# Squares of the latents summed by one-column matmuls in the second layer, and a last output block in narrower pieces

## The chip, the cores and the metric

The kernel runs as one program on one core of a Trainium2 chip. The metric is the device time of one execution in microseconds (us). The five engines named below are PE (TensorE, the matmuls), DVE (VectorE), ACT (ScalarE), POOL (GpSimd) and SP (SyncE, which here only starts DMAs). The kernel before was timed at 1753.45, 1750.38 and 1753.22 us, a median of 1753.22 us.

## The reference

Two layers of one mixer each, on a sequence of 1024 tokens of 1024 values. Per layer:

```
h = x * (1 + scale) + shift                      # scale, shift, gate from the conditioning c
p = h @ w_in                                     # split in latents, heads B, heads C, indexer, gates
cq  = rms_norm(p_cq)   (768 columns)             # x * rsqrt(mean(x*x) + 1e-6) * g
ckv = rms_norm(p_ckv)  (256 columns)
o_a = causal attention of 6 heads made from cq, ckv       (MLA, heads A)
o_b = causal dilated attention of 6 heads                 (heads B)
o_c = causal attention of 4 heads over the 256 best keys of each query (heads C, chosen by the indexer)
y   = concat(o_a, o_b, o_c) * silu(p_gate)
x   = layer_norm(ALPHA * x + (1 + gate) * (y @ w_out)) * ln_g + ln_b
```

The part of the change is the mean of squares in the two `rms_norm`, and the last layer norm of the last block of 128 tokens.

## The kernel before, in words

The products keep nearly the full precision of float32: every operand is split in a rounded high part and a low rest, and each product is three matmuls (`three`, L205; `chain`, L200, records them all under L204). A projection (`project`, L209) is two chains of 24 matmuls of 512 columns, one for each half of the tokens, each into a bank of the pool `ps_p` (name `pj`, two buffers); a nested function `evac` empties the bank by ACT and DVE. Other banks are `S` (scores, three buffers) and `T` (transposes, two buffers).

A layer runs: indexer scores; two early jobs; heads B; the selection of 256 keys (`select`, L470); heads C; the MLA heads; the output projection. The jobs are eight `latent` projections (i = 0, 1 for `ckv`, whose sums of squares go to `rk`; i = 2 to 7 for `cq`, whose sums go to `scq`) and three gate projections, handed out between the heads by the tables FB and FC. The selection is a search over 31 bits: in each round DVE counts three blocks (L467), ACT counts three others (L485), and DVE joins the two (L490 to L496). Heads B run beside it.

What one half of a `latent` job does (L610 to L626): ACT and DVE split the projected columns in `hi` and `lo`, and ACT writes the squares to `sq`, 128 latent columns by 512 tokens. The sum over the latent columns goes over partitions, so PE transposes `sq` in four pieces into a `T` bank (L619), and DVE adds along the free axis (L622 or L625) and, for all but the first chunk, adds the four numbers per partition to the running sums (L626).

In the output projection (`out_proj`, L811) each block of 128 tokens (order TBO: 7 down to 0) takes two chains of 24 matmuls of 512 columns. Behind each chain DVE multiplies by the gate row (L868), adds the residual (L869) and takes statistics (L870). Behind the second one the statistics are joined (L872, L874, POOL's L875), and in the last layer both halves are scaled and sent out by SP (L879 to L881).

The order of each engine's instructions is not the order of the code. `TileContext` is told to schedule (`schedule_with_timeline_sim=True`): it simulates the program while it is recorded and sets the order on every engine from that, so a change at one place can move instructions behind it.

Of the kernel before, what the change touches and what calls it, by code (L numbers as in the profile page):

```python
# [8 lines left out]
F32 = mybir.dt.float32  # L9
# [3 lines left out]
AF = mybir.ActivationFunctionType  # L13
OP = mybir.AluOpType
# [6 lines left out]
S = 1024  # L21
P = 128
# [13 lines left out]
TBO = (7,6,5,4,3,2,1,0)  # L36
# [72 lines left out]
def trunk(ctx: ExitStack, tc: tile.TileContext, a, out):  # L109
    nc = tc.nc  # L110
    pe, act, dve, pool, sp = nc.tensor, nc.scalar, nc.vector, nc.gpsimd, nc.sync

    sb = ctx.enter_context(tc.tile_pool(name="sb", bufs=1))
    small = ctx.enter_context(tc.tile_pool(name="small", bufs=3))
    ps_p = ctx.enter_context(tc.tile_pool(name="ps_p", bufs=2, space=PSUM))
    ps_s = ctx.enter_context(tc.tile_pool(name="ps_s", bufs=3, space=PSUM))
    ps_t = ctx.enter_context(tc.tile_pool(name="ps_t", bufs=2, space=PSUM))
# [8 lines left out]
    def fresh(tag, dtype, n=1024):  # L126

        return sb.tile([P, n], dtype, name=tag, tag=tag, bufs=1)
# [20 lines left out]
    ones = sb.tile([P, 1], F32, name="ones")  # L149
# [40 lines left out]
    def bc(t):  # L190
        return t.bitcast(F32)
# [17 lines left out]
    def project(wh, wl, nk, acts, evac, cuts=(0, 512, 1024)):  # L209

        for half in range(len(cuts) - 1):
            cols = slice(cuts[half], cuts[half + 1])
            bank = ps_p.tile([P, 512], F32, name="pj")
            ps = bank[:, :cols.stop - cols.start]
            items = []
            for k in range(nk):
                ws = slice(k * P, (k + 1) * P)
                items += three(wh[:, ws], wl[:, ws], acts[k][0][:, cols], acts[k][1][:, cols])
            chain(ps, items)
            evac(half, cols, ps)  # L220
# [3 lines left out]
    def w_chunk(l, i):  # L224
        return split_w(a["wt"][l, i], 1024)
# [378 lines left out]
    def latent(l, i):  # L604

        wh, wl = w_chunk(l, CKV + i)
        g = gkv[:, i:i + 1] if i < 2 else gq[:, i - 2:i - 1]
        sums = rk if i < 2 else scq

        def evac(half, cols, ps):  # L610
            hi, lo, sq = RW.next().bitcast(F32R), RW.next().bitcast(F32R), PR.next()
            act.activation(hi, ps, AF.Copy, scale=g)
            dve.scalar_tensor_tensor(lo, ps, g, bc(hi), OP.mult, OP.subtract)
            act.activation(sq, ps, AF.Square)
            for e, part in enumerate((hi, lo)):
                sp.dma_start(cq_d[:, (2 * i + e) * 1024 + half * 512:(2 * i + e) * 1024 + half * 512 + 512], bc(part))
            t = ps_t.tile([P, 4, P], F32, name="T")
            for j in range(4):
                pe.transpose(t[:, j, :], sq[:, j * P:(j + 1) * P], ident)  # L619
            to = sums[:, half * 4:half * 4 + 4]  # L620
            if i in (0, 2):
                dve.tensor_reduce(to, t, AX.X, OP.add)  # L622
            else:
                s4 = small.tile([P, 4], F32, name="s4")
                dve.tensor_reduce(s4, t, AX.X, OP.add)  # L625
                dve.tensor_tensor(to, to, s4, OP.add)  # L626

        project(wh, wl, 8, HA, evac)
        if i == 1:
            norm_r(rk, rk, 256, 1e-6, 1.0)  # L630
        elif i == 7:
            norm_r(scq, scq, 768, 1e-6, -float(96 ** -0.5))
# [11 lines left out]
    def norm_r(dst, src, n, eps, mul):  # L644

        dve.tensor_scalar(dst, src, 1.0 / n, eps, OP.mult, OP.add)
        pool.tensor_tensor(dst, dst, mhalf.to_broadcast(list(dst.shape)), OP.pow)
        if mul != 1.0:
            dve.tensor_scalar(dst, dst, mul, None, OP.mult)
# [160 lines left out]
    def out_proj(l):  # L810
        last = l == DEPTH - 1  # L811
        order = [3, 4, 5, 6, 7, 0, 1, 2]
        Y = HA
        for k in order[:5]:
            raw = WR.next()
            sp.dma_start(raw, y_d[k])
            act.activation(Y[k][0], raw, AF.Copy)
            (pool if k in YP[l] else dve).tensor_tensor(Y[k][1], raw, bc(Y[k][0]), OP.subtract)  # L818


        Vs = [VS[0][:, i * 1024:(i + 1) * 1024] for i in range(6)]
        f = G.n % 2 ^ 1
        XR = Ring([AC[0], RES] + ([G.tiles[f]] if last else []))
        at = {3: (Vs[4], Vs[5]), 4: (Vs[0], Vs[1]), 5: W.tiles[0:2], 6: W.tiles[2:4],
              7: (fresh(f"g{1 - f}", F32R), fresh("bi1", F32R)), 0: held[0:2], 1: held[2:4],
              2: (Vs[2], [fresh(f"rw{n}", F32R, 512) for n in range(2)])}
        wo = {}
        for k in order:
            raw = WR.next()
            sp.dma_start(raw, a["w_out"][l, k])  # L830
            hi, lo = at[k]
            eng = pool if k in WP[l] else dve
            for n in range(2):
                c = slice(n * 512, n * 512 + 512)
                act.activation(hi[:, c], raw[:, c], AF.Copy)  # L835
                eng.tensor_tensor(lo[n] if k == 2 else lo[:, c], raw[:, c], bc(hi[:, c]), OP.subtract)
            wo[k] = [(hi[:, n * 512:n * 512 + 512], lo[n] if k == 2 else lo[:, n * 512:n * 512 + 512]) for n in range(2)]
        g1 = BI.tiles[0]
        sp.dma_start(g1, g1_d[l].to_broadcast([P, 1024]))
        if last:  # L840
            sp.dma_start(LNG, a["ln_g"][l].to_broadcast([P, 1024]))
            sp.dma_start(LNB, a["ln_b"][l].to_broadcast([P, 1024]))
        else:

            lnc = small.tile([P, 2, 8], F32, name="lnc", bufs=1)
            sp.dma_start(lnc, a["ln_c"])
            dve.tensor_tensor(lnc[:, 0, :], lnc[:, 0, :], scale1_n, OP.mult)
            dve.tensor_tensor(lnc[:, 1, :], lnc[:, 1, :], scale1_n, OP.mult)
            dve.tensor_tensor(lnc[:, 1, :], lnc[:, 1, :], shift_n, OP.add)
        X = Ring(AC[1:4] + [PR3[0]])  # L850
        PR.tiles = [G.tiles[f]]
        xs = {}
        for tb in TBO:
            tok = slice(tb * P, (tb + 1) * P)
            xr = XR.next()
            sp.dma_start(xr, xw_d[tb] if last else a["x"][tb])
            r = X.next()
            st = small.tile([P, 2, 6], F32, name="st")
            for n in range(2):
                cols = slice(n * 512, n * 512 + 512)  # L860
                ps = (ps_p if n else ps_s).tile([P, 512], F32, name="pj" if n else "S")
                items = []
                for k in order:
                    yh, yl = Y[k]
                    w0, w1 = wo[k][n]
                    items += [(yh[:, tok], w0), (yl[:, tok], w0), (yh[:, tok], w1)]
                chain(ps, items)
                dve.tensor_tensor(r[:, cols], ps, g1[:, cols], OP.mult)  # L868
                dve.scalar_tensor_tensor(r[:, cols], xr[:, cols], ALPHA, r[:, cols], OP.mult, OP.add)  # L869
                dve.bn_stats(st[:, n, :], r[:, cols])  # L870
            mv = small.tile([P, 2], F32, name="mv")
            dve.bn_aggr(mv, st)  # L872
            rs = small.tile([P, 1], F32, name="rs")
            dve.tensor_scalar(rs, mv[:, 1:2], 1e-5, None, OP.add)  # L874
            pool.tensor_tensor(rs, rs, mhalf, OP.pow)  # L875
            if last:
                for n in range(2):
                    cols = slice(n * 512, (n + 1) * 512)
                    dve.scalar_tensor_tensor(r[:, cols], r[:, cols], mv[:, 0:1], LNG[:, cols], OP.subtract, OP.mult)  # L879
                    dve.scalar_tensor_tensor(r[:, cols], r[:, cols], rs, LNB[:, cols], OP.mult, OP.add)  # L880
                    sp.dma_start(out[tb][:, cols], r[:, cols])  # L881
                continue
            dve.tensor_scalar(r, r, mv[:, 0:1], rs, OP.subtract, OP.mult)
            sp.dma_start(x1_d[tb], r)
            xs[tb] = r
            if len(xs) == 4:
                for k in range(8):
                    t = ps_t.tile([P, 512], F32, name="T")
                    for j in range(4):
                        pe.transpose(t[:, j * P:(j + 1) * P], xs[tb // 4 * 4 + j][:, k * P:(k + 1) * P], ident)  # L890
                    mod_h(t, tb // 4, k, PR.next(), lnc[:, 0, :], lnc[:, 1, :])
                xs = {}
# [193 lines left out]
```

## Time and profile before

| what | value |
|---|---|
| timed runs | 1753.45, 1750.38, 1753.22 us (median 1753.22) |
| profiled execution, its own time | 1750.43 us |
| its span, first to last instruction | 1748.6 us |
| PE busy | 1673.0 us (96%) |
| DVE busy | 1350.5 us (77%) |
| ACT busy | 1019.8 us (58%) |
| POOL busy | 666.9 us (38%) |
| mean granted TensorE clock | 0.985 of full speed |

The second layer begins near 960 us of the span: the indexer's scores run until about 1046 us, the search of the selection from there to 1257 us with heads B beside it (the masks made from it until about 1402 us), heads C until about 1500 us, the MLA heads until about 1650 us, and the output projection to the end. The time outside the span, 1750.43 - 1748.6 = 1.8 us, is there in every execution.

### The profile page before, as it was taken

What the parts mean: (1) busy time and instruction counts of PE and PEld (TensorE: products, weight loads), DVE (VectorE), ACT (ScalarE), POOL (GpSimd) and SP (SyncE); (2) the same over time, 40 slices, a digit from 0 to 9 for tenths busy, and PEclk for the clock granted to TensorE, in tenths of its full rate; (3) what the DMA queues carried; (4) which work ended last, traced back from release to release, by engine and by line L of the source; (5) the groups of instructions that cost most, each with busy time, mean ns of one, the idle gap of its engine ahead of it and who ended that gap; (6) DMA issues with size and microseconds to landing.
All of it is one profiled execution on the core that took longest, in us unless ns stands there. A gap on an engine that the chain in (4) does not pass through costs nothing.

```text
span 1748.6 us, 26930 instructions
## 1 busy us (share of the span) xinstructions
PE 1673.0 (96%) x9192; PEld 1451.5 (83%) x9192; DVE 1350.5 (77%) x3213; ACT 1019.8 (58%) x2010; POOL 666.9 (38%) x614
## 2 busy tenths in 40 slices
PE   8999899999999999989999999999999899998998
PEld 8888688888887888878898977888789788987886
DVE  6888898888588678885772668889876967778777
ACT  4254599895534666675112656999744357667620
POOL 0221143323434355463346413333243344657421
PEclk9999999999999999999999999999999999999999
DMA  9665023233202521222343421333221227113122
GB/s 367 212 215 189 25 73 97 70 136 91 79 35 54 221 90 58 73 70 93 125 157 124 168 73 49 85 111 95 73 97 50 60 52 265 47 52 124 49 86 95
DMA packets 57668, 187.32 MB, mean 107 GB/s; under 512 B 7862, under 2 KB 8886, under 8 KB 57020
## 3 DMA queue, kind: packets, MB, share of 16 engines
q1 hardware_dynamic: 53116, 156.25, 26.3%
q0 software_dynamic: 4416, 29.36, 5.8%
q8 instruction: 72, 1.18, 0.3%
q14 instruction: 64, 0.52, 0.1%
HBM read 133.94 MB, written 39.07 MB: 99 GB/s over the span
## 4 chain that ended last, share of the span: by engine, by line
PE 53%; DVE 8%; ACT 3%; issue 2%; DMA 1%; POOL 1%; DVEq 0%; ACTq 0%; POOLq 0%
PE pj L204 30%; PE S L204 12%; PE O L332 5%; PE T L320 5%; DVE pt L324 1%; ACT pt L323 1%; PE T L204 1%; ACT scr L485 1%; DVE acc L543 0%; DVE pr L536 0%; DVE acc L441 0%; PE T L890 0%; DVE h L818 0%; DVE acc L291 0%; ACT pr L296 0%
## 5 line engine op out<-in xcount | busy, mean ns | idle before, releaser
L204 PE MATMUL pj<-h,w 128*128 128x512 f32 (+1 forms) x3408 | 833.0, 391 | 13.9 <-DVE qk L238 5.8
L204 PEld LDWEIGHTS pj<-h,w 128*128 128x128 f32 x3408 | 629.9, 190 | 131.1 <-issue 11.9
L198 POOL TENSOR_TENSOR w<-wr,w 128x1024 fp32r<-128x1024 f32 (+2 forms) x86 | 192.4, 2238 | 302.3 <-ACT w L197 290.1
L204 PE MATMUL S<-qk,qk 128*128 128x512 f32 (+2 forms) x1104 | 279.7, 358 | 8.4 <-DVE mx L288 3.1
L323 ACT ACTIVATE pt<-T 128x512 fp32r<-128x512 f32 (+1 forms) x320 | 172.4, 551 | 111.2 <-PE T L320 53.8
L298 POOL TENSOR_SCALAR pr<-pr,den 128x896 f32<-128x896 f32 (+7 forms) x180 | 139.0, 776 | 253.3 <-DVE den L297 223.9
L324 DVE TENSOR_TENSOR pt<-T,pt 128x512 fp32r<-128x512 f32 (+1 forms) x320 | 199.5, 633 | 43.9 <-ACT pt L323 37.9
L332 PE MATMUL O<-pt,v 128*128 128x256 f32 (+1 forms) x1280 | 212.8, 286 | 9.2 <-DVE pt L324 4.1
L485 ACT ACTIVATE scr<-acc,U 128x768 uint8<-128x768 f32 x186 | 193.2, 1038 | 35.6 <-DVE U L481 18.1
L204 PEld LDWEIGHTS S<-qk,qk 128*128 128x128 f32 x1104 | 184.2, 190 | 33.4 <-DVE mx L288 6.4
L332 PEld LDWEIGHTS O<-pt,v 128*128 128x128 f32 x1280 | 186.1, 191 | 26.7 <-DVE pt L324 6.7
L339 POOL TENSOR_TENSOR g<-g,osum 64x256 f32<-64x256 f32 x128 | 98.9, 773 | 235.0 <-DVE osum L337 222.8
L296 ACT ACTIVATE pr<-pr,mx 128x384 f32<-128x384 f32 (+7 forms) x188 | 145.5, 775 | 48.1 <-DVE mx L288 31.2
L320 PE MATMUL T<-ident,pr 128*128 128x128 f32 x852 | 145.4, 279 | 6.3 <-POOL pr L298 3.1
L467 DVE TENSOR_SCALAR_CACHE_REDUCE scr<-acc,U 128x384 uint8<-128x384 f32 x186 | 138.2, 743 | 3.8
L197 ACT ACTIVATE w<-wr 128x1024 fp32r<-128x1024 f32 (+2 forms) x86 | 83.8, 976 | 69.2 <-PE pj L204 59.7
L320 PEld LDWEIGHTS T<-ident,pr 128*128 128x128 f32 x852 | 102.1, 142 | 18.7 <-POOL pr L298 4.2
L204 PE MATMUL pj<-w,h 128*128 128x256 f32 (+2 forms) x672 | 107.0, 300 | 0.2 <-ACT w L835 0.2
L204 PEld LDWEIGHTS pj<-w,h 128*128 128x128 f32 x672 | 91.7, 190 | 5.1 <-ACT w L835 0.5
L336 ACT ACTIVATE osum<-O 64x256 f32<-64x256 f32 x128 | 48.6, 380 | 63.4 <-PE O L332 60.3
L441 DVE SCALAR_TENSOR_TENSOR acc<-S,wi,acc 128x512 f32<-128x512 f32 (+1 forms) x84 | 55.7, 678 | 23.0 <-ACT S L436 22.8
L337 DVE TENSOR_TENSOR osum<-O,osum 64x256 f32<-64x256 f32 x128 | 53.5, 418 | 25.1 <-ACT osum L336 21.4
(282 smaller groups left out, 2512.2 us busy)
## 6 DMA issues: line engine op xcount, KB each, us to landing
wr<-in_wt_dram SPq DMA_DIRECT2D x62, 512.0 KB, 3.9
cq_d<-rw SPq DMA_DIRECT2D x64, 256.0 KB, 2.0
h<-cq_d POOLq DMA_DIRECT2D x4, 4096.0 KB, 19.1
qk<-qk POOLq DMA_DIRECT2D x48, 256.0 KB, 3.0
pt<-in_w_ada_dram SPq DMA_DIRECT2D x22, 512.0 KB, 4.7
wr<-in_w_out_dram SPq DMA_DIRECT2D x16, 512.0 KB, 3.5
bi<-in_bias_dram SPq DMA_DIRECT2D x14, 512.0 KB, 3.7
bi<-in_w_ada_dram SPq DMA_DIRECT2D x10, 512.0 KB, 4.4
```

What stands on the lines that cost most here:

```text
L197: act.activation(hi[:, :n], raw[:, :n], AF.Copy)
L198: (lo_eng or pool).tensor_tensor(lo[:, :n], raw[:, :n], bc(hi[:, :n]), OP.subtract)
L204: pe.matmul(ps, lhsT=l, rhs=r, start=(i == 0), stop=(i == len(items) - 1))
L296: act.activation(p[:, :n], p[:, :n], AF.Exp, bias=m, scale=-1.0, accum_out=den)
L298: (dve if ne[qb] else pool).tensor_scalar(p[:, :n], p[:, :n], den, 0.5, OP.mult, OP.mult)
L320: pe.transpose(t[:, c:c + P], p[j](2 * kp + kk), ident)
L323: act.activation(pt[:, 0, :n], t[:, :n], AF.Copy)
L324: dve.tensor_tensor(pt[:, 1, :n], t[:, :n], bc(pt[:, 0, :n]), OP.subtract)
L332: pe.matmul(o[:, oc], lhsT=vt(kb), rhs=pt[:, e, pc], start=(kb == 0 and e == 0), stop=(kb == 2 * g + 1 and e == 1), skip_group_check=True)
L339: pool.tensor_tensor(yc, yc, s[r0:r0 + 64], OP.mult)
L467: dve.tensor_scalar(scr8[:, :IDX_LEN[b]], scores(b), s, None, op, OP.add, accum_out=dst[:, b:b + 1])
L485: act.activation(scr[:, :IDX_LEN[b]], scores(b), AF.Sign, bias=U[:, b:b + 1].bitcast(F32), accum_out=cnt[:, b:b + 1])
```

## The change

In the first layer (`l` is 0) nothing is recorded differently. In the second layer the four transposes of a half of `sq` become four matmuls that take the same piece of `sq` as weights and the column of ones (`ones`, 128x1) as the moving operand; each writes one column of a `T` bank. ACT copies the four columns out, straight to the sums for the first chunk, else to a small tile `s4`, which POOL adds to the sums. In the last block of the last layer the second chain of 512 columns becomes two chains of 256, statistics are taken in pieces of 256, and the second half of the output is sent from ACT's queue.

```diff
             act.activation(sq, ps, AF.Square)
             for e, part in enumerate((hi, lo)):
                 sp.dma_start(cq_d[:, (2 * i + e) * 1024 + half * 512:(2 * i + e) * 1024 + half * 512 + 512], bc(part))
+            if l:
+                to = sums[:, half * 4:half * 4 + 4]
+
+                t = ps_t.tile([P, 512], F32, name="T")
+                for j in range(4):
+                    pe.matmul(t[:, j:j + 1], lhsT=sq[:, j * P:(j + 1) * P], rhs=ones, start=True, stop=True,
+                              skip_group_check=True)
+                if i in (0, 2):
+                    act.activation(to, t[:, 0:4], AF.Copy)
+                else:
+                    s4 = small.tile([P, 4], F32, name="s4")
+                    act.activation(s4, t[:, 0:4], AF.Copy)
+                    pool.tensor_tensor(to, to, s4, OP.add)
+                return
             t = ps_t.tile([P, 4, P], F32, name="T")
             for j in range(4):
                 pe.transpose(t[:, j, :], sq[:, j * P:(j + 1) * P], ident)
@@ out_proj
-            st = small.tile([P, 2, 6], F32, name="st")
-            for n in range(2):
-                cols = slice(n * 512, n * 512 + 512)
-                ps = (ps_p if n else ps_s).tile([P, 512], F32, name="pj" if n else "S")
+
+            end = last and tb == TBO[-1]
+            st = small.tile([P, 4, 6], F32, name="st4", bufs=1) if end else small.tile([P, 2, 6], F32, name="st")
+            for o, w in ((0, 512), (512, 256), (768, 256)) if end else ((0, 512), (512, 512)):
+                n, cols = o // 512, slice(o, o + w)
+                bank = (ps_p if n else ps_s).tile([P, 512], F32, name="pj" if n else "S")
+                ps, part = bank[:, :w], slice(o % 512, o % 512 + w)
                 items = []
                 for k in order:
                     yh, yl = Y[k]
                     w0, w1 = wo[k][n]
-                    items += [(yh[:, tok], w0), (yl[:, tok], w0), (yh[:, tok], w1)]
+                    items += [(yh[:, tok], w0[:, part]), (yl[:, tok], w0[:, part]), (yh[:, tok], w1[:, part])]
                 chain(ps, items)
                 dve.tensor_tensor(r[:, cols], ps, g1[:, cols], OP.mult)
                 dve.scalar_tensor_tensor(r[:, cols], xr[:, cols], ALPHA, r[:, cols], OP.mult, OP.add)
-                dve.bn_stats(st[:, n, :], r[:, cols])
+                if end:
+                    for i in range(o, o + w, 256):
+                        dve.bn_stats(st[:, i // 256, :], r[:, i:i + 256])
+                else:
+                    dve.bn_stats(st[:, n, :], r[:, cols])
@@ out_proj, the last layer's output
-                    cols = slice(n * 512, (n + 1) * 512)
+                    cols, queue = slice(n * 512, n * 512 + 512), act if end and n else sp
...
-                    sp.dma_start(out[tb][:, cols], r[:, cols])
+                    queue.dma_start(out[tb][:, cols], r[:, cols])
```

The scheduler leaves the first layer's order alone and sets much of the second layer's anew. Two places on DVE are shown. The first is where the indexer of the second layer ends: `qk` tiles are the first B heads' queries and keys, read from the `pj` banks (L231 and L238), L467 are the first counts of the selection. Before, the two reduces of `rk` stand ahead of the first L238:

```order
L622 TENSOR_REDUCE rk<-T 128x4
L467 TENSOR_SCALAR scr,cnt_127<-acc 128x512
L231 TENSOR_TENSOR qk_82<-pj,qk_82 64x512
L441 SCALAR_TENSOR_TENSOR acc<-S,wi,acc 128x512
L446 TENSOR_TENSOR acc<-acc,causb 128x128
L622 TENSOR_REDUCE rk<-T 128x4
L238 TENSOR_TENSOR qk_76<-pj,qk_83 64x512
L467 TENSOR_SCALAR scr,cnt_127<-acc 128x640
L625 TENSOR_REDUCE s_9534<-T 128x4
L238 TENSOR_TENSOR qk_76<-pj,qk_83 64x512
```

The same place of the changed kernel on DVE:

```order
L467 TENSOR_SCALAR scr,cnt_127<-acc 128x512
L231 TENSOR_TENSOR qk_82<-pj,qk_82 64x512
L441 SCALAR_TENSOR_TENSOR acc<-S,wi,acc 128x512
L446 TENSOR_TENSOR acc<-acc,causb 128x128
L238 TENSOR_TENSOR qk_76<-pj,qk_83 64x512
L467 TENSOR_SCALAR scr,cnt_127<-acc 128x640
L238 TENSOR_TENSOR qk_76<-pj,qk_83 64x512
```

The reduces are gone and nothing took their place, so the first L238 follows the same neighbours two instructions earlier. On ACT the copies out of the `T` banks stand around the two L237 that feed these L238 (changed kernel, ACT, same place):

```order
L229 ACTIVATE qk_82<-pj 64x512
L436 ACTIVATE S<-S 128x512
L625 ACTIVATE rk<-T 128x4 x2
L237 ACTIVATE qk_83<-pj 64x512
L628 ACTIVATE s_9534<-T 128x4
L237 ACTIVATE qk_83<-pj 64x512
L628 ACTIVATE s_9572<-T 128x4
```

Before, the two L237 followed that L436 directly; the first two copies now stand ahead of both.

The second place is the end of the selection, beside head B's last projection (`qk_81`, `qk_83`) and the softmax of `pr_93`. Before, on DVE, a whole round of the selection (L490 here, the next at the end of the search) still follows the first L238:

```order
L238 TENSOR_TENSOR qk_83<-pj,qk_82 64x512
L288 ISA pr_93,mx<-S,bi_8696 128x384
L288 ISA mx 128x1
L625 TENSOR_REDUCE s_11047<-T 128x4
L467 TENSOR_SCALAR scr,cnt<-acc,U 128x640
L625 TENSOR_REDUCE s_11085<-T 128x4
L337 TENSOR_TENSOR osum<-O,osum 64x256
L288 ISA pr_93,mx<-S,bi_8696,mx 128x256
L288 ISA mx 128x1
L626 TENSOR_TENSOR scq<-scq,s_11047 128x4
L490 TENSOR_TENSOR pas<-cnt,tv 128x6
L626 TENSOR_TENSOR scq<-scq,s_11085 128x4
```

The changed kernel on DVE, from the same L238:

```order
L238 TENSOR_TENSOR qk_83<-pj,qk_82 64x512
L288 ISA pr_93,mx<-S,bi_8696 128x384
L288 ISA mx 128x1
L490 TENSOR_TENSOR pas<-cnt,tv 128x6
L288 ISA pr_93,mx<-S,bi_8696,mx 128x256
L288 ISA mx 128x1
L495 TENSOR_SCALAR mb<-pas 128x6
L508 MEMSET cnt 128x6
L337 TENSOR_TENSOR osum<-O,osum 64x256
L496 TENSOR_TENSOR U<-U,mb 128x6
```

L495 and L496 are the last round's, so with respect to the projections the selection's last round stands one round earlier than before.

## Rows read from the trace of the kernel before

**Rows 1.** Stretches: length, busy us (count) of PE, PEld, DVE, ACT, POOL; clock; DMA.
```profile
1056.00:1242.00 186.00, 185.55 (x954) 157.77 (x954) 159.05 (x474) 168.57 (x326) 63.25 (x61) 0.99 0.29 87
1242.00:1262.00 20.00, 17.30 (x85) 13.59 (x84) 19.18 (x55) 15.57 (x29) 7.01 (x8) 0.90 0.21 66
1262.00:1740.00 478.00, 463.54 (x2682) 403.44 (x2680) 362.46 (x852) 243.60 (x503) 210.06 (x214) 0.99 0.27 89
```

**Rows 2.** PE's waits, 1000 to 1740 us: total us, times, longest.
```profile
PE T L320 <- DVE pt L324: 5.6, 3, 5.0
PE T L619 <- DVE rk L622: 3.9, 2, 2.2
...
PE T L619 <- DVE acc L441: 1.2, 1, 1.2
```

**Rows 3.** Timeline, end of the indexer: start, duration, what, [idle before <-releaser].
```profile
1053.18 0.68 DVE L622 TENSOR_REDUCE rk<-T 128x4 f32<-128x512 f32 x1
...
1053.89 0.69 DVE L238 TENSOR_TENSOR qk<-pj,qk 64x512 fp32r<-64x512 f32 x1
1053.92 1.11 PE L619 MATMUL T<-ident,pr 128*128 128x128 f32 x4 [2.24 <-DVE rk L622]
...
1054.68 5.62 PE L204 MATMUL pj<-h,w 128*128 128x512 f32 x13
```

**Rows 4.** Stretches of 2 us behind it (columns as in rows 1).
```profile
1055.00:1057.00 2.00, 2.00 (x7) 1.52 (x6) 1.91 (x5) 0.00 (x0) 0.00 (x0) 0.50 0.26 51
```

**Rows 5.** Chain that ended last, 1220 to 1275 us: start, us, what.
```profile
1245.41 0.60 DVE s L625
...
1246.81 0.61 DVE s L625
...
1248.38 1.57 DVE scq L626
...
1250.03 0.61 DVE scq L626
```

**Rows 6.** Timeline of the same stretch, POOL and PE.
```profile
1247.53 2.40 POOL L198 TENSOR_TENSOR w<-wr,w 128x1024 fp32r<-128x1024 f32 x1 [6.02 <-ACT w L197]
```

**Rows 7.** PE's timeline behind the selection.
```profile
1261.20 6.35 PE L204 MATMUL pj<-h,w 128*128 128x512 f32 x20
```

**Rows 8.** ACT's waits, 1056 to 1242 us.
```profile
ACT scr L485 <- DVE U L493: 6.6, 8, 1.7
```

**Rows 9.** Smallest ACT and nearest POOL operations, from the groups by form.
```profile
L250 ACT ACTIVATE cs<-ccol 128x8 f32<-128x8 f32 x1 | 0.2, 209 | 0.3 <-DMA ccol<-in_c_dram 0.3
L366 ACT ACTIVATE v<-pj,rk 128x128 fp32r<-128x128 f32 x16 | 5.6, 364 | 1.3 <-PE pj L204 1.2
...
L298 POOL TENSOR_SCALAR pr<-pr,den 128x128 f32<-128x128 f32 x20 | 8.2, 410 | 24.6 <-DVE den L297 19.8 <-DVE scq L626 4.7
```

**Rows 10.** PE's timeline: four transposes of squares in a full stream.
```profile
1177.29 0.60 PE L619 MATMUL T<-ident,pr 128*128 128x128 f32 x4
1177.64 1.17 PE L204 MATMUL pj<-h,w 128*128 128x512 f32 x4
```

**Rows 11.** PE's timeline in the kernel's beginning: sixteen one-column matmuls.
```profile
25.93 1.84 PE L925 MATMUL O<-cs,g 128*128 128x1 f32 x16
27.63 0.61 PE L911 MATMUL pj<-qk,h 128*128 128x392 f32 x2
```

**Rows 12.** Chain that ended last: values of heads C, 24 matmuls of 256 columns.
```profile
1358.60 2.88 PE pj L204 x24
```

**Rows 13.** Chain that ended last, the kernel's end.
```profile
1734.71 5.45 PE pj L204 x24
...
1740.19 0.70 DVE pr L868
...
1742.37 0.22 DVE mv L872
```

**Rows 14.** DVE's groups by form: a 256-column operation on a bank.
```profile
L364 DVE TENSOR_TENSOR v<-pj,v 128x256 fp32r<-128x256 f32 x16 | 6.5, 414 | 0.6 <-ACT v L363 0.3
```

## The prediction

> **What bounds the kernel now.** I read the busy times first, then PE's waits in the second layer, the timeline around each long one, and the chain that ended last at those places. Only the second layer is in question, since the order of the first stays as it is. PE is the bound nearly everywhere in it: while the selection searches, PE is busy 185.55 of 186 us, DVE 159.05 and ACT 168.57 [rows 1]. Work taken from DVE there is worth nothing by itself. It is worth something only where PE waits, and the waits are few: 2.7 us of the 20 us behind the search and 14.5 of the next 478 us [rows 1], and at the end of the indexer 3.9 and 1.2 us in front of the transposes that are replaced (L619) [rows 2]. So I price the two places at which DVE's reduces and adds stand between PE and its next work, then PE's own exchange, then the kernel's end.
>
> **End of the indexer.** Sixteen transposes (two `latent` jobs, two halves, four each) stand here in a row. With two `T` banks the third and the fourth group wait until DVE has reduced the first two. In the changed kernel ACT empties those banks, and ACT has little else there. But the next thing PE does is a projection into a `pj` bank, and that bank is read last by DVE's L238, from 1053.89 to 1054.58; PE's chain starts at 1054.68 [rows 3]. So PE exchanges one wait for another: the bank, not the transposes, is late next. What moves is L238 itself: two reduces of 0.68 us [rows 3] no longer stand ahead of it on DVE, as the order shows, which is 1.4 us. Behind the idling the granted clock is 0.50 of full speed, the lower of its two levels, 1.2 GHz [rows 4], and 13 matmuls take 5.62 us [rows 3], where 24 take 5.45 us at the end of the kernel [rows 13], 0.227 each, 2.95 for 13. That loss of 2.7 us I leave in, because PE still idles until L238. Bounds: nothing, if the copies that now stand ahead of L237 on ACT hold it up; or -7.8 us, if all of 5.1 us of waiting and the 2.7 us go. I take -1.4, the row of the reduces.
>
> **End of the search.** Here the chain that ended last runs over DVE, and four of its pieces are what the change removes: 0.60, 0.61, 1.57 and 0.61 us [rows 5], 3.4 us together. PE idles 2.7 us in this stretch [rows 1], and then runs 20 matmuls in 6.35 us [rows 7] instead of 20 x 0.227 = 4.5, so 4.5 us are at stake. The order adds that the last round of the search now comes one round earlier relative to the projections, so that less DVE work is packed in here. Against it stands ACT, which is busy 91% of the search [rows 1] and gets ten copies of four numbers before the search ends. No row shows such a copy: one of 128x8 takes 209 ns and one of 128x128 from a bank 364 ns [rows 9]; I take 0.21, nearest in size, so ten are 2.1 us and sixteen 3.4 us. ACT also waits 6.6 us in the search for DVE [rows 8], and with six reduces and their adds fewer on DVE before the last of these rounds part of that comes back. I let 0.4 us of the copies through to the end of the search: -3.4 + 0.4 = -3.0 us. Bounds: -4.5, all that is at stake, and +3.6, ten copies at 364 ns with nothing given back.
>
> The longest of the four pieces, an add of 4 numbers per partition in 1.57 us, starts while POOL's 2.40 us operation runs and ends with it, at 1249.95 against 1249.93 us [rows 5, 6]. The Trainium skill, GPSIMD Engine Reference, "Specifications", gives the reason and a caution: POOL's access to SBUF is shared with VectorE and contends with DVE operations that have two SBUF inputs, so adds that move to POOL would meet DVE still. By that rule the two adds here would give back 2 x 0.41 = 0.8 us, the nearest POOL operation [rows 9] being the estimate, and the sum would be -3.7 instead of -4.5.
>
> **PE's exchange.** Sixteen groups. Four transposes in a full stream cost PE 1177.64 - 1177.29 = 0.35 us [rows 10]. Sixteen one-column matmuls in a row cost 27.63 - 25.93 = 1.70 us, 0.106 each [rows 11]; four are 0.43. So the exchange gains nothing: 16 x 0.08 = +1.2 us at most; or, if the first of four hides behind the matmul ahead of it, 3 x 0.106 = 0.32 and -0.5. I take +0.4, the middle.
>
> The Trainium skill, TensorE: Matmul & The Clock Gate, "Back-to-back issue gap", has a table in which matmuls of 1 to 64 columns stand at about 60 cycles, 25 ns. By it four would cost 0.10 us and the groups would gain 16 x 0.25 = 4.0 us. The row of 0.106 us says otherwise; the page's section "LDWEIGHTS (loading the stationary operand)" gives 107 ns for 128 columns of weights, and agrees with it.
>
> **The end.** Two chains of 24 matmuls of 256 columns replace one of 512. Heads C's values show 2.88 us for 24 of 256 columns [rows 12], so 5.76 against 5.45 us [rows 13]: +0.3. Behind the last matmul DVE's three steps take 1742.37 - 1740.19 = 2.18 us at 512 columns [rows 13]. A 256-column step takes 0.414 us [rows 14] and a gap of 0.03: three are 1.33, -0.85. The first piece's steps lie beside the second chain. No row has a DMA started by ACT; before, SP starts the second half only when DVE has finished it, so the other queue removes no wait, and I allow 0.3 us either way. Together -0.5 us; bounds -1.2, and +0.6 if the statistics do not shrink with the width.
>
> **What moves without being changed.** From 1262 to 1740 us the order of PE is set anew at many places. PE's 14.5 us of waiting there include one of 5.0 us for DVE in the MLA heads [rows 1, 2]. It comes where DVE splits the rows of y for the output projection; in the new order these splits (L818) stand some ten instructions earlier on DVE, but as close together. I value the new order at nothing and bound it by half the waiting, 7 us, either way.
>
> **Sum.** -1.4 - 3.0 + 0.4 - 0.5 = -4.5 us against the profiled execution's own 1750.43 us (span 1748.6 and 1.8 around it): 1745.9. That execution is one of the two lower ones; the four known times, 1753.45, 1750.38, 1753.22 and 1750.43, have a mean of 1751.9, and from there it is 1747.4 us.
>
> **Rivals.**
> A. ACT becomes the bound of the search (slower). It is the busiest engine beside PE there, and every round ends on the later of DVE and ACT. If the ten copies fall ahead of L485 on ACT and cost 364 ns, the search ends 3.6 us later, the masks with it, and PE waits and then runs at 1.2 GHz as in rows 7, another 1.8 us. With -1.4, +0.4 and -0.5 that is +3.9 us, 1755.8. It decides once the copies cost ACT more than DVE's relief gives back of the 6.6 us [rows 8]. Against it: PE has other heads' work to run while the search is late.
> B. The relief is off the path or another wait takes its place, so that only the small terms are left or the new order eats them: about 1751.5. For it speaks that PE is full, and that 14.5 us of waits lie where the order is new.
> C. Both stalls go with their slow stretches: -7.8 - 4.5 + 0.4 - 0.5 = -12.4, 1739.5. For it speaks how full DVE is in both; against it the bank that L238 holds.
> D. One-column matmuls cost a fraction of a transpose. At a quarter of the 0.106 us of rows 11 the groups would gain 16 x 0.25 = 4.0 instead of losing 0.4: 1743. The row speaks against it. This is the table of the page named above.
>
> **How the numbers follow.** Forecast 0.47, A 0.13, B 0.20, C 0.17, D 0.03. The forecast's own range is 1743 to 1751. For 8 in 10 the range takes in C's edge and A: 1739 to 1756. About 0.2% is what a measurement of this kernel can tell from no change, 3.5 us, or below 1749.7 against the median of 1753.22. Faster by more: 0.39 of the forecast's 0.47, C, D and a little of B, 0.60. Within it: 0.07 of the forecast and most of B, 0.24. Slower: A and the rest, 0.16.
>
> **What would show it.** L238 ends some 1.4 us sooner after the indexer's last score and PE's chain follows at once; at the end of the search PE's waits of 2.7 us shrink, and the slow stretch with them; four one-column matmuls take about 0.43 us of PE; the last DVE step before the joined statistics is 0.44 us long. It is wrong if ACT's rounds get longer, if new waits of several us stand after 1262 us, or if the first gap closes altogether.

## The result and the profile after

The changed kernel takes 1765.28 us (median of four runs, 1762.74 to 1765.6), the kernel before 1752.4 us beside it (1750.38 to 1753.45). The ratio is 1.0073, with a 95% interval of 1.006 to 1.0085: slower by 13 us. The prediction was 1747.4 us, 1739 to 1756, so it was wrong in sign and range. The profiled execution has a span of 1763.7 us (before: 1748.6). About 1.1 us of that difference arose in the first layer, whose order is the same: the first group of squares of the second layer starts at 1047.95 instead of 1046.86 us. Outside the span lie 1.8 us in both profiled executions, but up to 3.4 us in other executions of the kernel before, so it is not the same in every one. A few executions of e9, of e11 and of the kernel before beside them were far slower than the rest; the ratios leave them out.

**PE has more to do.** The busy line of the page after; the last number is the count of records:

```profile
PE 1687.0 (96%) x9280; PEld 1468.7 (83%) x9280; DVE 1342.9 (76%) x3189; ACT 1020.5 (58%) x2026; POOL 670.5 (38%) x626
```

PE is busy for 14 us more than the 1673.0 us of before, and it has 88 records more (9192 before). The end explains 24 of them, 48 matmuls for 24. The other 64 must come from the sums, though 64 matmuls replaced 64 transposes. The view of one line (records, minimum, median and maximum in ns, first and last start) tells how, first after, then the same view of the transposes before, and of the one-column matmuls at the beginning of the kernel, on whose price the prediction rests:

```profile
L622 PEld LDWEIGHTS T<-ones,pr x128: 186/192/338, 1047.9 to 1298.8; 128*128 128x128 f32 x128
L622 PE MATMUL T<-ones,pr x128: 164/251/353, 1048.0 to 1298.8; 128*128 128x1 f32 x128
```
```profile
L619 PE MATMUL T<-ident,pr x128: 270/273/477, 192.4 to 1294.2; 128*128 128x128 f32 x128
...
L925 PE MATMUL O<-cs,acc x64: 164/297/373, 5.4 to 45.8; 128*128 128x1 f32 x64
```

L619 stands for 64 transposes in each of the two layers, 128 records for 128 instructions. L622 stands for 64 instructions, four in each of 16 groups, and also has 128 records: a float32 matmul with one moving column is carried out as two weight loads and two matmuls. L925 shows the same: eight instructions in the loop over `c`, four times with weights from a tile `acc`, 32 instructions and 64 records. The x16 of [rows 11] were therefore eight instructions, at 0.21 us each. The timeline shows the price in a full stream, in answer to [rows 10]:

```profile
1184.64 0.95 PE L622 MATMUL T<-ones,pr 128*128 128x1 f32 x8
1185.44 0.96 PE L204 MATMUL pj<-h,w 128*128 128x512 f32 x3
1186.24 0.95 PE L622 MATMUL T<-ones,pr 128*128 128x1 f32 x8
1187.05 1.86 PE L204 MATMUL pj<-h,w 128*128 128x512 f32 x7
```

From the start of a group to the start of what follows it takes 0.80 and 0.81 us, where four transposes took 0.35 [rows 10].

**The end of the indexer**, in answer to [rows 3]:

```profile
1047.95 1.05 PE L622 MATMUL T<-ones,pr 128*128 128x1 f32 x8
1049.42 4.83 PE L622 MATMUL T<-ones,pr 128*128 128x1 f32 x24 [0.41 <-ACT rk L625]
1054.53 2.08 PE L204 MATMUL pj<-h,w 128*128 128x512 f32 x4 [0.29 <-DVE qk L238]
```

The waits of 3.9 and 1.2 us [rows 2] are gone but for 0.41 us, and PE fills the time with its own records, which run 0.20 us apart at 1.2 GHz (the clock in the next fence). From the first group to the projection it is 1054.53 - 1047.95 = 6.58 us, before 1054.68 - 1046.86 = 7.82: a gain of 1.24 us.

**Stretches** (columns as in [rows 1]). The first three answer to [rows 1], with the end of the last matmul as the last bound; the fourth is the end of the indexer; the others are stretches behind 1302 us in which the granted clock is half:

```profile
1056.00:1242.00 186.00, 185.56 (x964) 158.28 (x963) 155.16 (x463) 171.39 (x338) 62.80 (x64) 0.99 0.28 87
1242.00:1262.00 20.00, 18.40 (x103) 15.43 (x101) 18.50 (x54) 12.13 (x26) 7.52 (x10) 1.00 0.17 50
1262.00:1756.00 494.00, 472.62 (x2724) 412.63 (x2724) 360.26 (x842) 244.32 (x508) 212.03 (x218) 0.98 0.26 87
...
1050.00:1052.00 2.00, 2.00 (x12) 2.00 (x11) 1.97 (x5) 0.77 (x2) 0.00 (x0) 0.50 0.00 0
...
1381.10:1384.30 3.20, 2.96 (x7) 2.39 (x8) 3.10 (x4) 0.00 (x0) 3.20 (x2) 0.50 0.51 175
1401.60:1404.80 3.20, 3.03 (x7) 2.48 (x8) 2.39 (x10) 2.02 (x5) 1.76 (x3) 0.50 0.80 164
1562.00:1565.20 3.20, 3.20 (x12) 2.81 (x11) 2.91 (x5) 1.57 (x3) 0.85 (x2) 0.50 0.50 173
1609.80:1613.00 3.20, 3.20 (x13) 3.07 (x13) 2.95 (x8) 2.52 (x5) 3.20 (x2) 0.50 0.38 138
1620.10:1626.70 6.60, 5.99 (x25) 5.53 (x26) 4.11 (x10) 4.32 (x10) 5.61 (x7) 0.50 0.39 120
```

Behind 1302 us the kernel before has two such stretches, of 3.4 and 6.8 us; after there are five, four of 3.4 and one of 6.8 us: 20.5 us instead of 10.2, and half of the difference, 5.1 us, is lost. Each comes behind a wait of PE. PE's waits from 960 us on (total, times, longest), in answer to [rows 2]:

```profile
PE T L320 <- DVE pt L324: 7.3, 6, 2.0
PE pj L204 <- DVE v L364: 4.3, 1, 4.3
PE pj L204 <- DVE qk L238: 3.1, 4, 2.4
```

**What PE waits for there** shows in the chain that ended last around the longest of them (start, us, what; PE idles from 1377.1 to 1381.3):

```profile
1375.86 1.03 DVE scr L542
1376.88 0.02 issue
1376.91 1.37 DVE acc L543
1378.28 0.03 issue
1378.31 2.65 DVE scr L532
1380.95 0.33 DVE v L364
```

Three operations of the masks (L542, L543, L532) stand on DVE ahead of the L364 that empties PE's bank, and the longest of them, L532, runs beside an operation of POOL. The timelines, after and then before:

```profile
1377.54 5.63 POOL L198 TENSOR_TENSOR w<-wr,w 128x1024 fp32r<-128x1024 f32 x2
```
```profile
1367.06 5.29 POOL L198 TENSOR_TENSOR w<-wr,w 128x1024 fp32r<-128x1024 f32 x2 [5.94 <-ACT w L197]
1370.41 2.36 DVE L532 TENSOR_SCALAR scr<-acc,thr 128x768 uint8<-128x768 f32 x1
...
1379.32 0.69 DVE L532 TENSOR_SCALAR scr<-acc,thr 128x896 uint8<-128x896 f32 x1
```

The L532 of 896 columns takes 2.65 us beside POOL's L198; before, POOL is idle beside it and it takes 0.69 us. Before, the L532 of 768 columns met L198 and took 2.36 us. In the second layer of all 13 traces this operation of the masks (other line numbers in e6 and e9) takes 2.0 to 2.9 us where it runs beside POOL's weight split for 1.5 us or more, and 0.41 to 0.76 us elsewhere. So L364 was late before too, 3.9 us behind ACT's copy of the same bank against 4.2 now. But before, PE had score matmuls to run in between and idled 0.7 and 2.1 us; now it idles 4.3.

**The end of the search.** The last round's L496 starts at 1248.34 instead of 1256.63 us; from the first group of squares that is 200.4 instead of 209.8 us, 9.4 us sooner. PE's timeline behind it:

```profile
1261.26 0.55 PE L320 MATMUL T<-ident,pr 128*128 128x128 f32 x3 [1.40 <-POOL pr L298]
1262.89 0.74 PE L204 MATMUL S<-qk,qk 128*128 128x512 f32 x2 [1.08 <-DVE mx L288]
1265.14 1.97 PE L332 MATMUL O<-pt,v 128*128 128x256 f32 x8 [1.51 <-DVE osum L337]
```

PE waits 4.0 us all the same (2.7 before, [rows 1]). The chain shows what DVE did in between, and the timelines what ran beside it, after and then before:

```profile
1249.87 0.67 DVE K L503
...
1251.18 1.02 DVE scr L467 x2
1252.20 2.02 DVE K L512
1254.23 1.06 DVE scr L467 x2
```
```profile
1251.80 2.40 POOL L198 TENSOR_TENSOR w<-wr,w 128x1024 fp32r<-128x1024 f32 x1 [1.27 <-ACT w L197]
```
```profile
1264.19 0.16 DVE L512 TENSOR_TENSOR K<-K,Kb 128x6 int32<-128x6 int32 x1
```

The counts behind the last round (L503 to L512, with L467) do not shrink with the change. PE's stall no longer stands around the last round but 12 to 17 us behind it, among these counts. And the meeting of DVE with POOL's L198 moved: it no longer stretches an L626 to 1.57 us [rows 5, 6] but the L512, to 2.0 us instead of 0.16.

**The end**, in answer to [rows 13], from the chain that ended last:

```profile
1750.21 5.76 PE pj L204 x48
...
1756.00 0.44 DVE pr L885
...
1757.38 0.27 DVE mv L893
```

48 matmuls take 5.76 us, and DVE's three steps 1757.38 - 1756.00 = 1.38 us. From the start of the last chain to the end of the span it is 13.5 us, before 13.9.

**The account.** I took PE from the first group of squares to its last matmul in both traces, and added up the gaps between its records and the time at 1.2 GHz, of which half is lost. Before: 693.3 us, of which 22.7 idle and 11.9 lost to the clock, so 658.6 of work at full clock. After: 708.0, 24.1, 17.1, 666.9. Of +14.7 us, 8.2 are work, 5.1 the clock, 1.4 idling; -0.8 behind the last matmul. The same account stands below for the experiments; traces of one and the same work differ in their work by up to 2.5 us (before and e4), once by 4.5 (e6 and e9).

### The profile page after: what moved, and what is told of

Same layout as the page of the kernel before. It is cut to its first block, busy times and chain, and to the rows that moved or that the text cites. A ratio compares the mean times of both kernels' runs of the same rounds, so it can differ in the third digit from the quotient of the medians.

```text
span 1763.7 us, 27119 instructions
## 1 busy us (share of the span) xinstructions
PE 1687.0 (96%) x9280; PEld 1468.7 (83%) x9280; DVE 1342.9 (76%) x3189; ACT 1020.5 (58%) x2026; POOL 670.5 (38%) x626
## 4 chain that ended last, share of the span: by engine, by line
PE 51%; DVE 8%; ACT 4%; issue 3%; DMA 2%; POOL 1%; DVEq 0%; ACTq 0%; POOLq 0%
PE pj L204 29%; PE S L204 11%; PE O L332 5%; PE T L320 4%; DVE pt L324 1%; ACT scr L485 1%; DMA h<-cq_d 1%; ACT pt L323 1%; DVE scr L467 1%; DVE pr L536 1%; ACT pr L296 1%; PE T L204 1%; PE T L622 0%; DVE acc L441 0%; DVE scr L541 0%
## 5 line engine op out<-in xcount | busy, mean ns | idle before, releaser
L198 POOL TENSOR_TENSOR w<-wr,w 128x1024 fp32r<-128x1024 f32 (+2 forms) x86 | 192.7, 2242 | 308.0 <-ACT w L197 297.4
L467 DVE TENSOR_SCALAR_CACHE_REDUCE scr<-acc,U 128x384 uint8<-128x384 f32 x186 | 138.3, 743 | 3.8
```

The source lines that it names most:

```text
L198: (lo_eng or pool).tensor_tensor(lo[:, :n], raw[:, :n], bc(hi[:, :n]), OP.subtract)
L467: dve.tensor_scalar(scr8[:, :IDX_LEN[b]], scores(b), s, None, op, OP.add, accum_out=dst[:, b:b + 1])
```

## Experiments

Theories. P: the one-column matmuls in float32 cost PE twice what the prediction took. O: the new order of the second layer brings waits of its own and stretches at 1.2 GHz behind them. Rivals: all is price; or the cost is the handing over to ACT and POOL; or the end costs. Ratios are against the kernel before, run beside each, five rounds.

**e1_tail: the end alone.** Against the changed kernel the sums go back to their old code; the order up to the last block is that of before.

```diff
-            if l:
-                to = sums[:, half * 4:half * 4 + 4]
...
-                return
```

> Only the last block's edit (two chains of 256 columns, statistics in pieces of 256, second half sent from ACT's queue); the sums stay as before, and every engine's order up to the last block with them. Theory E1, as the prediction had it: the time from the start of the last chain's columns to the end of the span falls from 13.9 to 13.4 us, so the kernel is 0.4 to 0.5 us faster than before, ratio 0.9997. Rival: the second queue and the doubled number of matmuls cost more than the short statistics give, and the end is longer, +0.5 us or more.

Measured: 0.9993 (0.9984 to 1.0002), medians 1750.55 and 1751.62 us. That fits -0.5 and does not show it, since the interval holds no change. The trace does: behind the last matmul 7.7 us instead of 8.5, the chains 0.3 us longer. The end is not where the 13 us come from.

**e2_price_col and e3_price_tr: the price by itself.**

```diff
                 chain(ps, items)
+                if last and not (tb == TBO[-1] and n):
+                    t = ps_t.tile([P, 512], F32, name="T")
+                    for j in range(4):
+                        pe.matmul(t[:, j:j + 1], lhsT=ident, rhs=ones, start=True, stop=True, skip_group_check=True)
```

e3 has `pe.transpose(t[:, j * P:(j + 1) * P], ident, ident)` in the last line.

> The kernel before with 15 extra groups of four float32 one-column matmuls (weights: the identity, moving: the column of ones) behind 15 of the 16 chains of the last output projection, into a T bank that nobody reads; the order of the rest stays. Theory P (each instruction is two weight loads and two matmuls, 0.21 us; a group 0.81 to 0.86 us in a full stream): +12.4 us, 15 x 0.83. The price on record in the prediction (0.106 each, 0.43 a group): +6.4 us. If the groups fit between the chains at no cost: 0.

> The same with 15 groups of four transposes of the identity in place of the one-column matmuls. Theory P: 15 x 0.35 = +5.3 us, 7 us less than the run with one-column matmuls. The price on record: +5.3 us as well, but only 1.2 us less than that run.

Measured: 1.007 (1.0054 to 1.0086), 1764.36 against 1751.62 us, +12.7; and 1.0038 (1.0023 to 1.0053), 1758.57 us, +7.0 where both theories had 5.3, inside the interval of 4.0 to 9.3. The first answers 12.4, not 6.4; the difference of 5.8 us is nearer to 7 than to 1.2. The timelines, e2 and then e3, each with the start of what follows:

```profile
1727.56 0.95 PE L871 MATMUL T<-ones,ident 128*128 128x1 f32 x8
1728.37 1.65 PE L204 MATMUL S<-v,h 128*128 128x512 f32 x6
```
```profile
1728.04 0.60 PE L871 MATMUL T<-ident 128*128 128x128 f32 x4
1728.40 1.64 PE L204 MATMUL S<-v,h 128*128 128x512 f32 x6
```

Four one-column matmuls are 8 records and 0.81 us, four transposes 4 records and 0.36 us. Theory P holds: 0.45 us a group.

**e4_swap_before: another order, the same work.**

```diff
+            if l:
+                act.activation(sq, ps, AF.Square)
             act.activation(hi, ps, AF.Copy, scale=g)
             dve.scalar_tensor_tensor(lo, ps, g, bc(hi), OP.mult, OP.subtract)
-            act.activation(sq, ps, AF.Square)
+            if not l:
+                act.activation(sq, ps, AF.Square)
```

> The kernel before with one edit that changes no work: in the second layer's latent jobs ACT is given the square ahead of the copy with scale. The same instructions, but the schedule of the second layer comes out anew. Theory O (a new order of the second layer by itself brings or takes waits of 2 to 4 us and the stretches at 1.2 GHz behind them): the time moves by 2 to 7 us either way, and its waits and low-clock stretches account for it. Rival: the order is worth little, the time stays within 2 us of before, and all of the 13 us of the change are the one-column matmuls' own price.

Measured: 0.9959 (0.9944 to 0.9974), 1744.39 against 1751.62 us, -7.2. The stretch at the end of the search, in answer to [rows 1]:

```profile
1242.00:1262.00 20.00, 20.00 (x112) 17.10 (x111) 18.66 (x59) 15.62 (x31) 6.79 (x7) 1.00 0.28 80
```

PE has no gap and full clock there (the last round is at 1253.1), with the old transposes and DVE's reduces and adds. So the order alone closes the stall for which the prediction had priced DVE's work. The account: 686.4 us, 20.1 idle, 10.2 lost to the clock, 656.1 of work. Of the -6.9 us in it, idling and clock explain 4.3; the 2.5 of work I can't assign.

**e5_swap_after: the change in another order.** The same edit on the changed kernel.

> The changed kernel with the square ahead of the copy with scale on ACT in the second layer's latent jobs, the edit of e4_swap_before. Work and price of the change stay: 16 groups at 0.45 us more than transposes, +7.2 us, and the narrow end, -0.5. Theory O (the rest of the 13 us is this order of the second layer, not the work): the time moves by 2 us or more from the 1765.3 us of the changed kernel, and lies between -2 and +14 us of before, 6.7 us being price and end alone. Rival (the rest is inherent in the change, ACT and POOL behind the sums): it stays within 2 us of the changed kernel, ratio to before 1.0065 to 1.0085.

Measured: 1.0026 (1.0016 to 1.0036), 1756.59 against 1751.56 us, +5.0. The same work as the change, 8 us less. From the first group of squares to the last matmul: 696.6 us, 22.3 idle, 8.5 lost to the clock, 665.8 of work. The work is that of the changed kernel (666.9); the clock gives 8.5 us back and the idling 1.8. That stretch is 11.4 us shorter, more than the 8, because the first layer took 3.3 us longer in this execution. Theory O holds, and "all is price" falls.

**e6_bf16: cheap one-column matmuls.**

```diff
+            if l:
+                sq = sq.bitcast(BF16)[:, 0:512]
...
+    ones_b = sb.tile([P, 1], BF16, name="ones_b")
+    dve.memset(ones_b, 1.0)
...
-                    pe.matmul(t[:, j:j + 1], lhsT=sq[:, j * P:(j + 1) * P], rhs=ones, start=True, stop=True,
+                    pe.matmul(t[:, j:j + 1], lhsT=sq[:, j * P:(j + 1) * P], rhs=ones_b, start=True, stop=True,
```

> The changed kernel with the squares and the column of ones kept in bfloat16 for these sums (less precise sums), so that each piece should be one weight load and one matmul. Theory P: the records of the 64 instructions are 64 and not 128, a group in a full stream takes 0.43 us or less and not 0.82, and the price against transposes goes from 7.2 to 1.3 us or less; the schedule comes out anew, so the total is known only to the size of an order, 1752 to 1759 with 1758 if the waits of the changed kernel stay. Rival (the price lies elsewhere, on ACT and POOL): the time stays at +13 us, 1765.

Measured: 0.9989 (0.9978 to 1.0001), 1749.88 against 1751.56 us. PE's timeline, two groups in a stream, and then the end of the indexer:

```profile
1176.39 0.35 PE L626 MATMUL T<-ones_b,pr 128*128 128x1 bf16 x8
1176.61 1.63 PE L206 MATMUL pj<-h,w 128*128 128x512 f32 x6
...
1048.45 0.35 PE L626 MATMUL T<-ones_b,pr 128*128 128x1 bf16 x8 [0.26 <-ACT rk L629]
1053.14 2.08 PE L206 MATMUL pj<-h,w 128*128 128x512 f32 x4 [4.34 <-DVE qk L240]
```

Eight records now are eight instructions and take 0.22 us, 0.11 a group. It also shows how far the relief at the indexer reaches: PE is done with the sums at once and then waits 4.34 us for L240 (L238 of before) to empty the bank, as the prediction said of that bank: the projection starts 6.66 us behind the first group, in the changed kernel 6.58. The time lies 2 us below the 1752 to 1759 expected. ACT and POOL copy and add as in the changed kernel, so the rival that puts the cost on them falls. The account: 691.1 us, 26.8 idle (the 4.34 among it), 10.2 lost to the clock, 654.1 of work. That is 4.6 us less work than before, where the groups should save 4.0 against transposes, and 12.8 less than in the changed kernel, where 16 x 0.71 = 11.4 are due. Behind 1302 us PE idles nearly as long as in the changed kernel (18.7 and 18.9 us), but only 10.2 us there are at 1.2 GHz, against 20.5.

**e7_early and e11_late: a part of the groups.** `if l:` becomes `if l and i < 2:` in e7 and `if l and i > 1:` in e11.

> The change with its sums by one-column matmuls only in the two latent jobs at the end of the indexer (4 of the 16 groups); the six others keep transposes and DVE's reduces; with the narrow end. Theory: PE's 5.1 us of waiting in front of these transposes go, the four groups cost more at 1.2 GHz, and DVE's L238, which holds the projection's bank, comes 1.2 us sooner: -1.2 there, -0.5 at the end, and a new order of the rest, which may be worth as much as the 7 us of e4_swap_before: 1742 to 1757 with 1750 as the middle. Rival: PE's waits were worth their full 5.1 us, and the time falls by 5 us or more with no new long wait behind 1300 us.

> The change with one-column sums only in the six latent jobs behind the indexer (12 of 16 groups); the two jobs at the indexer's end keep transposes and DVE's reduces; with the narrow end. Theory P: PE's work at full clock is 12 x 0.45 + 0.3 = 5.7 us above before, PE's 5.1 us of waiting at the indexer's end are back, the search's end is worth at most 3 us, and the order of the rest is worth up to 8 us either way: 1749 to 1765. If the indexer's end was where the change lost most, the time is at 1755 or below.

Measured: e7 1.0047 (1.003 to 1.0064), 1761.43 against 1751.56 us; e11 1.0054 (1.004 to 1.0067), 1761.42 against 1752.32. Four groups alone cost 10 us, which no price explains: 4 x 0.45 = 1.8. PE's waits of e7 behind 1300 us:

```profile
PE T L320 <- DVE pt L324: 7.3, 6, 2.0
PE pj L204 <- DVE v L364: 4.3, 1, 4.3
PE pj L204 <- DVE qk L238: 2.6, 2, 2.4
```

They are those of the changed kernel, and so is the time at 1.2 GHz behind 1302 us, 20.5 us. So both expectations failed for e7: mine was 1742 to 1757 with 1750 as the middle. The work is 662.4 us in e7 and 666.9 in e11, and before 1302 us e7 loses 1.7 us more to the clock than the changed kernel. It is the order, which came out behind 1302 us as in the changed kernel, that costs most. e11 lies in its range, with PE's waits at the indexer's end back (1.20, 1.64 and 2.24 us); its work is 8.3 us above before where 5.7 were expected.

**e8_swap_tail: the better order with the narrow end.** The edits of e4 and e1 together.

> The kernel before with the square ahead of the copy (e4_swap_before) and the narrow last block (e1_tail), transposes kept. The order up to the last block is that of e4_swap_before, so both add: -7.2 - 0.5 = -7.7 us against before, ratio 0.9956. Rival: the end does not add, 0.9960 or more.

Measured: 0.995 (0.9934 to 0.9966), 1743.74 against 1751.56 us, -7.8. It beats both kernels, but the interval holds the 0.9956 of the theory and the 0.9960 of its rival, so it does not show that the end adds. The account: 685.2 us, 20.6 idle, 6.8 lost to the clock, 657.7 of work.

**e9_swap_bf16 and e10_dve_copies.** e9 joins e4's edit with e6. e10 replaces ACT and POOL behind the sums:

```diff
-                    act.activation(to, t[:, 0:4], AF.Copy)
+                    dve.tensor_copy(to, t[:, 0:4])
...
-                    act.activation(s4, t[:, 0:4], AF.Copy)
-                    pool.tensor_tensor(to, to, s4, OP.add)
+                    dve.tensor_copy(s4, t[:, 0:4])
+                    dve.tensor_tensor(to, to, s4, OP.add)
```

> The bfloat16 sums of e6_bf16 with the square ahead of the copy and the narrow end (less precise sums). A group of one-column matmuls costs 0.11 us there, so the work is 16 x (0.36 - 0.11) = 4 us less than with transposes. If the waits are those of e8_swap_tail (-7.8 us against before): -12 us, 1740. If they are those of e5_swap_after (+5.0): 5.0 - 16 x (0.82 - 0.11) = -6.4 us, 1745. Rival: a new order again, with its own waits, up to the 1750 of e6_bf16.

> The changed kernel with DVE in place of ACT and POOL for the copies of four numbers and the adds behind the one-column matmuls. Theory P: PE's busy time at full clock stays 8 us above before (7.2 price, 0.3 the end), since the 128 records stay; the rest is order: 1752 to 1766. Rival (the cost of the change is the handing over to ACT and POOL): the time falls to 1753 or below, and PE's work with it.

Measured: e9 1.003 (1.0019 to 1.0041), 1757.59 against 1752.32 us, a miss of 13 us against the 1745 expected at most, and of 8 against the rival's bound: with a new order it idles 31.3 us where e6 idles 26.8 (in a trace of 1752.14 us, the fastest of its executions, so not a typical one), and e4's edit, worth -7.2 us on the kernel before, is worth +7 on e6. So that edit isn't good in itself; it draws another order. e10: 1.0036 (1.0021 to 1.005), 1759.3 us, work 665.4: with DVE in place of ACT and POOL PE's work stays some 7 us up, as theory P has it.

## Why the prediction was wrong

- **End of the indexer: right.** -1.4 predicted, -1.24 found, by the step named: the bank that L238 holds is late next, and without two reduces ahead of it it comes that much sooner. The price of the four groups there lies inside the time in which PE would have waited; e6 shows that wait (4.34 us). That was in part luck: the groups, mispriced and at 1.2 GHz, were done only 0.29 us before the bank was free.
- **End of the search: the mechanism failed, -3.0 predicted, about 0 found.** DVE's pieces [rows 5] are gone and the search ends 9.4 us sooner, counted from the first group. But PE waits 1.3 us more in the 250 us behind the first group, apart from the indexer's gap, and 2.9 us less of them are at 1.2 GHz, 1.5 us gained. The next work on DVE, the counts behind the last round, took the place of the reduces. The term was also too large by the 1.57 us of an add, which the prediction saw end with POOL's L198 and counted as gone: in the new order L198 met the L512, which took 2.0 us instead of 0.16. The prediction should have asked what stands behind the search on DVE, and who of PE's softmax steps queues there. Rival A did not come: a copy on ACT takes 0.15 to 0.17 us, less than the 0.21 taken, and the search ends sooner, not later.
- **PE's exchange: mis-sized, +0.4 predicted (at most +1.2), +5.5 found.** The failing step is "four are 0.43": it took the x16 of [rows 11] for sixteen instructions. They are two records each; a group takes 0.81 us in place of 0.35. Twelve groups stand in a full stream: 12 x 0.45 = 5.4; in the trace group by group 5.5. e2 and e3 show the price by itself. The Trainium skill, TensorE: Matmul & The Clock Gate, "Back-to-back issue gap", gives some 25 ns for up to 64 columns. In bfloat16 the trace of e6 agrees (0.22 us for eight); in float32 that of the changed kernel does not (0.10 us for each of two records), so rival D, which rests on it, did not come.
- **The end: right in the trace.** -0.5 predicted; 13.5 for 13.9 us there. The times of e1 can't tell it from nothing.
- **What moves without being changed: the largest failure, 0 predicted, bounded by 7, +9.6 found.** The failing step is "I value the new order at nothing". Behind 1302 us PE idles 18.9 us instead of 14.5, and 5.1 us more are lost at 1.2 GHz behind the new waits. The bound was half of the waiting, and left out the clock: a wait of 2 us behind which 3.4 us run at half speed costs 3.7. That it is the order is shown by e5 (the same work, 8 us less), e7 (a quarter of the groups, the same waits, +10 us) and e4 (no change of work, -7.2 us). The prediction's own sign of being wrong, new waits of several us after 1262 us, came with the 4.3 us at L364. What makes one order dearer than another is settled only in part: the traces show which operations met (L532 and POOL's L198) and what PE had left to run, but no run changed that alone.

The terms found, -1.2 - 0.2 + 5.5 - 0.5 + 9.6, make +13.2 us; the medians differ by 12.9, the two traces from the first group on by 13.9, so 0.7 us of the trace stay unassigned.

## What to carry to other kernels

Compare the count of records of a row with the count of instructions in the code before taking a price from it; two records per instruction doubled this one. Where a scheduler sets the order, an edit in the middle of a program is worth its own price and a draw of a new order, here from -7.2 (e4) to +9.6 us (the change), so size that draw with an edit that changes no work, and price a wait with the stretch at 1.2 GHz behind it. When a search or a chain ends sooner, ask what its engine does next before counting the gain.

## What the runs showed of the hardware

- A float32 matmul with one moving column is two weight loads and two matmuls, 0.20 to 0.21 us; in bfloat16 it is one of each and 0.03 us, and a float32 transpose of 128 columns is one of each and 0.09 us.
- DVE operations ran several times longer beside POOL's L198, which splits weights: L532 on 896 columns 2.65 us beside it and 0.69 without, L512 on six columns 2.0 us and 0.16. So POOL, busy 38% of the span, can hold up a bank that PE waits for, and the order decides which DVE operation it meets.
- At the end of the indexer PE idled only 0.41 us between its one-column matmuls from 1047.95 us on, and yet the granted clock fell to half (0.50 at 1050 to 1052). In e2 three rows of sixteen such records, with chains of 512 columns between them, left it at full:

```profile
1684.00:1697.00 13.00, 13.00 (x87) 11.77 (x86) 12.78 (x26) 0.80 (x2) 3.91 (x4) 1.00 0.48 162
```

- With the same order of the first layer, the second layer's first group of squares starts anywhere from 1046 us (e9) to 1053 us (e3) in the profiles, so a place in two traces is compared from a common event and not from the start of the span.
